# Rotary embedding on one core: all transfers of x on one DMA ring, in the order of the work

## The chip, the core and the metric

One core of a Trainium2 chip runs the kernel. The metric is device time in microseconds (us) of one execution; the kernel before has a median of 161.87 us over three runs (161.72 to 161.93).

## The reference

x is float32 of shape (16, 512, 1024): 16 batches, 512 positions, 16 heads of 64 columns. cos and sin are (512, 32).

```python
x = x.reshape(batch, seq, num_heads, head_dim)
x1, x2 = x[..., :half_dim], x[..., half_dim:]
cos = cos[None, :, None, :]
sin = sin[None, :, None, :]
rotated = np.concatenate([x1 * cos - x2 * sin,
                          x1 * sin + x2 * cos], axis=-1)
```

33.55 MB are read and 33.55 MB written.

## The kernel before

**Tiles.** A slab is two batches' worth of x, 4.19 MB: 128 partitions with 8 rows of 1024 floats each (8192 floats a partition). There are eight slabs, 0 to 7. Two neighbours make a pair, and three places in on-chip memory hold a pair each, so slabs 6 and 7 reuse the place of slabs 0 and 1. `here(s, n)` is the place of `n` slabs from slab `s` on, `there(t, s, n)` the same slabs in the input or output.

**Loads.** SyncE issues them, on its own ring (L65 in `load`, and L83). In program order: load 0, load 1, slabs 2-3 as two transfers (even partitions, then odd), then slabs 4-5 as one transfer of 8.39 MB (L84). None of these has to wait. Load 6 and load 7 are written behind store 0 and store 1 and wait for them, since they overwrite their places.

**Tables.** ScalarE issues the loads of cos and sin (L78). GpSimd casts them to bf16 (L99), TensorE spreads them over the partitions (L106), VectorE and ScalarE copy the result into two bf16 tables.

**Work on a slab.** It goes in passes: one pass for most slabs, two for slab 0, three for slab 7. ScalarE casts the slab to bf16 in place (`cast`, which calls `copy`, L138), VectorE does two multiplications with the tables (L152) and one addition with the halves swapped (L155), ScalarE copies the result back to float32 in place (`copy` again). ScalarE's copies are kept in the order in which they are written: the cast of the next slab comes ahead of the copy back of this one, and all casts of slab 7 come ahead of the copy back of slab 6. So its order is cast 0 in two parts, cast 1, copy 0 in two parts, cast 2, copy 1, cast 3, copy 2, cast 4, copy 3, cast 5, copy 4, cast 6, copy 5, cast 7 in three parts, copy 6, copy 7 in three parts.

**Stores.** ScalarE issues them on its own ring, between its copies: stores 0 to 3 singly (L69 in `store`), slabs 4-5 as two transfers behind copy 5 (L162), slabs 6-7 as one of 8.39 MB at the end (L69).

An engine works off its own instructions in order. A transfer that waits for a copy or for another transfer makes its issuing engine wait; a transfer that is issued runs by itself. So the loads of slabs 0 to 5 are on SyncE's ring from the start, and the stores come in from ScalarE's ring as they are ready.

Of the kernel before, what the change touches and what calls it, by code (L numbers as in the profile page):

```python
# [2 lines left out]

# [4 lines left out]


@with_exitstack  # L10
def kernel(
    ctx: ExitStack,
    tc: tile.TileContext,
    x: bass.AP,
    cos: bass.AP,
    sin: bass.AP,
    num_heads: int,
    out: bass.AP,
):
    nc = tc.nc  # L20
    P = nc.NUM_PARTITIONS

    batch, seq, dim = x.shape
    nh = num_heads
    hd = dim // nh
    half = hd // 2
    bf16 = mybir.dt.bfloat16
    f32 = mybir.dt.float32

    nb = 2  # L30
    nslabs = batch // nb
    rpp = nb * seq // P
    W = rpp * dim
    TP = seq // rpp
    TW = rpp * half

    out_flat = out.rearrange("b s h d -> b s (h d)")

    singles = ctx.enter_context(tc.tile_pool(name="singles", bufs=1))
    pairs = ctx.enter_context(tc.tile_pool(name="pairs", bufs=3))  # L40
    psum = ctx.enter_context(tc.tile_pool(
        name="psum", bufs=1, space=bass.MemoryType.PSUM))


    def view(t, offset, *dims):
        return dataclasses.replace(t, offset=t.offset + offset,
                                   ap=[t.ap[0], *[list(d) for d in dims]])

    places = [pairs.tile([P, 2 * W], f32, tag="pair", name="pair") for _ in range(3)]


    def here(s, n=1):
        return view(places[s // 2 % 3], s % 2 * W, (1, n * W))


    def there(t, s, n=1):
        return bass.AP(tensor=t.tensor, offset=t.offset + s // 2 * 2 * P * W + s % 2 * W,  # L60
                       ap=[[2 * W, P], [1, n * W]])


    def load(s, n=1):
        nc.sync.dma_start(out=here(s, n), in_=there(x, s, n))  # L65


    def store(s, n=1):
        nc.scalar.dma_start(out=there(out_flat, s, n), in_=here(s, n))  # L69


    load(0)


    cos_sb = singles.tile([TP, TW], f32, tag="cos_sb")
    sin_sb = singles.tile([TP, TW], f32, tag="sin_sb")
    for t, src in ((cos_sb, cos), (sin_sb, sin)):
        nc.scalar.dma_start(out=t, in_=bass.AP(  # L78
            tensor=src.tensor, offset=src.offset, ap=[[TW, TP], [1, TW]]))

    load(1)
    for p in range(2):
        nc.sync.dma_start(out=here(2, 2)[p::2], in_=there(x, 2, 2)[p::2])  # L83
    load(4, 2)  # L84


    pick = singles.tile([TP, 4 * P], bf16, tag="pick")
    nc.gpsimd.memset(pick, 0.0)  # L88
    for h in range(2):
        for g in range(2):  # L90
            part = view(pick, (2 * h + g) * P, (TP // 2, 2 * P // TP), (1, TP // 2))
            nc.gpsimd.affine_select(  # L92
                out=part, in_=part, compare_op=mybir.AluOpType.not_equal,
                fill=1.0 - 2.0 * g, base=-h, pattern=[[0, 2 * P // TP], [-2, TP // 2]],
                channel_multiplier=1)

    tab1 = singles.tile([TP, 2 * TW], bf16, tag="tab1")
    for i, t in enumerate((cos_sb, sin_sb)):
        nc.gpsimd.tensor_copy(out=view(tab1, i * TW, (1, TW)), in_=t)  # L99

    accs, tabs = [], []
    for h in range(2):
        acc = psum.tile([P, 2 * rpp * hd], f32, tag=f"acc{h}", name="acc")
        for i in range(2):
            for f in range(2):
                nc.tensor.matmul(  # L106
                    view(acc, i * rpp * hd + f * half, (hd, rpp), (1, half)),
                    view(pick, (2 * h + i * f) * P, (1, P)),
                    view(tab1, i * TW, (half, rpp), (1, half)),
                    start=True, stop=True)  # L110
        accs.append(acc)
        tabs.append(singles.tile([P, 2 * rpp * hd], bf16, tag=f"tab{h}", name="tab"))
    nc.vector.tensor_copy(out=tabs[0], in_=accs[0])  # L113

    passes = []
    for s in range(nslabs):
        r = 0  # L120
        for n in {0: (4, 4), nslabs - 1: (4, 2, 2)}.get(s, (rpp,)):
            passes.append((s, r, n))
            r += n


    def halves(u):
        s, r, n = u
        t = here(s).bitcast(bf16)
        return [view(t, (2 * r + i * n) * dim, (1, n * dim)) for i in range(2)]


    def cast(u):
        s, r, n = u
        copy(halves(u)[0], view(here(s), r * dim, (1, n * dim)))


    def copy(out, in_):
        tc.keep_in_program_order(nc.scalar.copy(out=out, in_=in_))  # L138


    ahead = list(passes)
    for _ in range(2):
        cast(ahead.pop(0))
    copy(tabs[1], accs[1])
    cast(ahead.pop(0))
    for i, u in enumerate(passes):
        s, r, n = u
        while ahead and len(passes) - len(ahead) < (i + 2 if s < nslabs - 2 else len(passes)):
            cast(ahead.pop(0))
        lo, up = halves(u)  # L150
        for t, a in ((up, 0), (lo, rpp * hd)):
            nc.vector.tensor_mul(  # L152
                out=t, in0=lo,
                in1=view(tabs[s % 2], a + r * hd, (hd, n), (0, nh), (1, hd)))
        nc.vector.tensor_add(  # L155
            out=up, in0=up, in1=view(lo, half, (hd, n * nh), (-half, 2), (1, half)))

        copy(view(here(s), r * dim, (1, n * dim)), up)
        if r + n == rpp:
            if s == 5:  # L160
                for p in range(2):
                    nc.scalar.dma_start(out=there(out_flat, 4, 2)[p::2], in_=here(4, 2)[p::2])  # L162
            elif s == 7:
                store(6, 2)
            elif s < 4:
                store(s)
            if s < 2:
                load(s + 6)


# [1 line left out]
_INS = ['x', 'cos', 'sin', 'num_heads']  # L172
_OUTS = [((16, 512, 16, 64), 'float32')]

_NUMBERS = {'num_heads': 16}


# [26 lines left out]
```

## Time and profile before

| | before |
|---|---|
| median of 3 runs | 161.87 us (161.72 to 161.93) |
| the profiled execution | 161.8 us, span 160.0 us |
| ScalarE busy | 114.3 us (71%) |
| VectorE busy | 107.9 us (67%) |
| TensorE busy | 2.0 us (1%) |
| GpSimd busy | 2.6 us (2%) |
| HBM read, written | 33.69 MB, 33.55 MB |
| mean over the span | 420 GB/s |
| a full cast or copy of a slab on ScalarE | 7.02 us |
| a full multiplication or addition on VectorE | 4.42 us |
| issue of a store on ScalarE | 0.34 us |

The span runs from the first to the last instruction of the profiled execution; its own time is 1.8 us longer. Busy times count work, not the issuing of transfers. Times within the profile are counted from the start of the span. Queue q1 is SyncE's ring, q10 ScalarE's.

### The profile page before, as it was taken

The numbers are of one execution on the slowest core, as the hardware profiler recorded it, in microseconds if no ns is written. First come the engines' busy times: TensorE is split into PE (matmuls) and PEld (weight loads), VectorE is DVE, ScalarE is ACT, GpSimd is POOL, SyncE is SP. The second block draws the span as 40 slices with busy tenths as digits, with TensorE's granted clock in tenths as the row PEclk, the third lists the DMA queues.
The fourth block names the chain that finished last, engine by engine and source line by source line (L and its number), as shares of the span: only waits on it lengthen the run. The fifth ranks groups of instructions, "written<-read, shape, count | busy, mean of one in ns | idle before, by whom it ended". The sixth has DMA issues, their size and how long they took to land.

```text
span 160.0 us, 167 instructions
## 1 busy us (share of the span) xinstructions
PE 2.0 (1%) x8; PEld 1.0 (1%) x8; DVE 107.9 (67%) x34; ACT 114.3 (71%) x24; POOL 2.6 (2%) x11
## 2 busy tenths in 40 slices
PE   0001300000000000000000000000000000000000
PEld 0000100000000000000000000000000000000000
DVE  0000499999951999799889979998999998000000
ACT  3006959993089989998998999999879999500000
POOL 4000000000000000000000000000000000000000
DMA  7999999699599999999999999999997999989966
GB/s 262 401 401 410 426 491 524 262 524 524 254 401 410 606 426 393 393 393 393 467 451 393 434 483 393 401 500 410 393 590 328 524 393 393 524 360 426 524 262 262
DMA packets 1920, 67.24 MB, mean 420 GB/s; under 512 B 256, under 2 KB 384, under 8 KB 384
## 3 DMA queue, kind: packets, MB, share of 16 engines
q1 hardware_dynamic: 880, 33.55, 49.5%
q10 hardware_dynamic: 1040, 33.69, 48.7%
HBM read 33.69 MB, written 33.55 MB: 420 GB/s over the span
## 4 chain that ended last, share of the span: by engine, by line
ACT 52%; DMA 26%; issue 5%; ACTq 1%; SPq 1%; another core or an unknown queue 0%
ACT pair L138 52%; DMA pair<-in_x_dram 26%; ACTq L162 1%; ACTq L69 1%; SPq L65 0%; SPq L83 0%; ACTq L138 0%
## 5 line engine op out<-in xcount | busy, mean ns | idle before, releaser
L138 ACT CAST pair<-pair 128x8192 bf16<-128x8192 f32 (+5 forms) x22 | 112.1, 5155 | 21.9 <-DMA pair<-in_x_dram 19.8
L152 DVE TENSOR_TENSOR pair<-pair,tab 128x8192 bf16<-128x8192 bf16 (+2 forms) x22 | 71.4, 3259 | 9.3 <-ACT pair L138 8.9
L155 DVE TENSOR_TENSOR pair<-pair 128x8192 bf16<-128x8192 bf16 (+2 forms) x11 | 35.8, 3260 | 0.3
L113 DVE CAST tab<-acc 128x1024 bf16<-128x1024 f32 x1 | 1.2, 1225 | 18.3 <-PE acc L106 18.3
L138 ACT ACT_TABLE_LOAD x1 | 1.3, 1283 | 2.0 <-issue 2.0
L106 PE MATMUL acc<-tab,pick 64*128 64x256 bf16 x8 | 2.0, 403 | 17.1 <-POOL tab L99 17.1
L106 PEld LDWEIGHTS <-pick 64*128 64x128 bf16 x8 | 1.0, 127 | 17.6 <-issue 15.6
L92 POOL TENSOR_SCALAR_AFFINE_SELECT pick<-pick 64x128 bf16<-64x128 bf16 x4 | 1.1, 303 | 0.1
L138 ACT CAST tab<-acc 128x1024 bf16<-128x1024 f32 x1 | 1.0, 1004 | 0.0
L99 POOL CAST tab<-cos_sb 64x256 bf16<-64x256 f32 x1 | 0.4, 391 | 9.5 <-DMA cos_sb<-in_cos_dram 9.5
L88 POOL MEMSET pick<- 64x512 bf16 x1 | 0.5, 519 | 0.3 <-POOLq L185 0.3
L99 POOL CAST tab<-sin_sb 64x256 bf16<-64x256 f32 x1 | 0.4, 396 | 4.9 <-DMA sin_sb<-in_sin_dram 4.9
L185 POOL MEMSET const-float32-0.0<- 128x1 f32 x1 | 0.1, 104 | 0.2 <-issue 0.2
L185 POOL MEMSET const-bfloat16-1.0<- 128x1 bf16 x1 | 0.1, 107 | 0.0
L185 POOL MEMSET const-uint8-127<- 128x1 uint8 x1 | 0.1, 107 | 0.0
L185 POOL MEMSET const-float32-1.0<- 128x1 f32 x1 | 0.1, 104 | 0.0
## 6 DMA issues: line engine op xcount, KB each, us to landing
pair<-in_x_dram SPq DMA_DIRECT2D x4, 4096.0 KB, 22.5
out_dram<-pair ACTq DMA_DIRECT2D x4, 4096.0 KB, 32.8
cos_sb<-in_cos_dram ACTq DMA_DIRECT2D x1, 64.0 KB, 11.1
sin_sb<-in_sin_dram ACTq DMA_DIRECT2D x1, 64.0 KB, 15.8
pair<-in_x_dram SPq DMA_DIRECT2D x3, 42.2
out_dram<-pair ACTq DMA_DIRECT2D x3, 21.0
```

The lines of the kernel that those rows point to most:

```text
L69: nc.scalar.dma_start(out=there(out_flat, s, n), in_=here(s, n))
L88: nc.gpsimd.memset(pick, 0.0)
L92: nc.gpsimd.affine_select(out=part, in_=part, compare_op=mybir.AluOpType.not_equal, fill=1.0 - 2.0 * g, base=-h, pattern=[[0, 2 * P // TP] ...
L99: nc.gpsimd.tensor_copy(out=view(tab1, i * TW, (1, TW)), in_=t)
L106: nc.tensor.matmul(view(acc, i * rpp * hd + f * half, (hd, rpp), (1, half)), view(pick, (2 * h + i * f) * P, (1, P)), view(tab1, i * TW, ( ...
L113: nc.vector.tensor_copy(out=tabs[0], in_=accs[0])
L138: tc.keep_in_program_order(nc.scalar.copy(out=out, in_=in_))
L152: nc.vector.tensor_mul(out=t, in0=lo, in1=view(tabs[s % 2], a + r * hd, (hd, n), (0, nh), (1, hd)))
L155: nc.vector.tensor_add(out=up, in0=up, in1=view(lo, half, (hd, n * nh), (-half, 2), (1, half)))
L162: nc.scalar.dma_start(out=there(out_flat, 4, 2)[p::2], in_=here(4, 2)[p::2])
L185: nc = _bacc.Bacc("TRN2", target_bir_lowering=False, num_devices=1)
```

## The change

Loads and stores of x are all issued by SyncE, so they all go through one ring, and they are kept in the order in which they are written. Store 0 stands ahead of the load of slabs 4-5. The order is: load 0, load 1, slabs 2-3 in two transfers, store 0, load 4-5, store 1, load 6, store 2, load 7, store 3, slabs 4-5 stored in two transfers, store 6-7. Loads 6 and 7 stood behind stores 0 and 1 in the program and stand behind stores 1 and 2 now. ScalarE issues only the tables. The copies, the multiplications and the places are what they were.

```diff
     def load(s, n=1):
-        nc.sync.dma_start(out=here(s, n), in_=there(x, s, n))
+        tc.keep_in_program_order(nc.sync.dma_start(out=here(s, n), in_=there(x, s, n)))
 
     def store(s, n=1):
-        nc.scalar.dma_start(out=there(out_flat, s, n), in_=here(s, n))
+        tc.keep_in_program_order(
+            nc.sync.dma_start(out=there(out_flat, s, n), in_=here(s, n)))
...
     load(1)
     for p in range(2):
-        nc.sync.dma_start(out=here(2, 2)[p::2], in_=there(x, 2, 2)[p::2])
-    load(4, 2)
+        tc.keep_in_program_order(
+            nc.sync.dma_start(out=here(2, 2)[p::2], in_=there(x, 2, 2)[p::2]))
...
             if s == 5:
                 for p in range(2):
-                    nc.scalar.dma_start(out=there(out_flat, 4, 2)[p::2], in_=here(4, 2)[p::2])
+                    tc.keep_in_program_order(nc.sync.dma_start(
+                        out=there(out_flat, 4, 2)[p::2], in_=here(4, 2)[p::2]))
             elif s == 7:
                 store(6, 2)
             elif s < 4:
                 store(s)
-            if s < 2:
-                load(s + 6)
+            if s < 3:
+                load(*((4, 2), (6,), (7,))[s])
```

## The prediction

> **What bounds the kernel now.** I read the table of DMA queues first, because the digits of the DMA row are nearly all 9.
>
> ```profile
> q1 hardware_dynamic: 880, 33.55, 49.5%
> q10 hardware_dynamic: 1040, 33.69, 48.7%
> HBM read 33.69 MB, written 33.55 MB: 420 GB/s over the span
> ```
>
> q1 carries SyncE's loads, q10 ScalarE's stores and tables. The packets of both fill 49.5 + 48.7 = 98.2% of 160.0 us, that is 157.1 us on each of the 16 DMA engines. The table of windows shows where the other 2.9 us lie (columns after the width: PE, PEld, DVE, ACT, POOL busy, clock, DMA share, GB/s; a packet is counted whole where it begins, so short windows overshoot).
>
> ```profile
> 1.60:1.70 0.10, 0.00 (x0) 0.02 (x1) 0.00 (x0) 0.00 (x0) 0.10 (x2) 1.00 0.00 0
> 1.70:2.20 0.50, 0.00 (x0) 0.08 (x1) 0.00 (x0) 0.21 (x1) 0.50 (x3) 1.00 3.75 1049
> 24.00:28.00 4.00, 0.00 (x0) 0.00 (x0) 4.00 (x3) 4.00 (x1) 0.00 (x0) 1.00 1.21 524
> 28.00:32.00 4.00, 0.00 (x0) 0.00 (x0) 3.96 (x3) 4.00 (x2) 0.00 (x0) 1.00 0.61 262
> 36.00:40.00 4.00, 0.00 (x0) 0.00 (x0) 3.97 (x2) 1.27 (x1) 0.00 (x0) 1.00 1.36 524
> 46.00:70.00 24.00, 0.00 (x0) 0.00 (x0) 17.77 (x5) 23.59 (x4) 0.00 (x0) 1.00 1.01 437
> 158.50:158.70 0.20, 0.00 (x0) 0.00 (x0) 0.00 (x0) 0.00 (x0) 0.00 (x0) 1.00 0.02 0
> 158.70:160.00 1.30, 0.00 (x0) 0.00 (x0) 0.00 (x0) 0.00 (x0) 0.00 (x0) 1.00 0.00 0
> ```
>
> The first packet begins at 1.7 us, the last near 158.6: 156.9 us that packets fill entirely. The engines of the chip's DMA never stand still; this is one stream, and the order in which its bytes go cannot shorten it. Only packets that took longer than their bytes need can. The rate without trouble is 524 GB/s at share 1.21, so 433 GB/s at share 1. Loads alone (24 to 28) have it, and so has the mixed stretch (46 to 70: 437 at 1.01). Three places show more time for the same bytes. 36 to 40 has 1.36 where 24 to 28 has 1.21 for 524 GB/s: 0.15 x 4 = 0.6 us. 0 to 4 has 0.77 (page, first slice, 262 GB/s) where 28 to 32 has 0.61: 0.6 us, the first bytes of the run. 12 to 16, beside the tables, has 1.02 at 410 GB/s where 48 to 52 has 0.95: 0.3 us. 67.24 MB at 433 GB/s is 155.3 us; with 0.6 + 0.6 + 0.3 it is 156.8 of the 157.1 counted, so 0.3 us is unassigned.
>
> The chain of waits puts ScalarE first; its end says why that is an accident.
>
> ```profile
> ACT 52%; DMA 26%; issue 5%; ACTq 1%; SPq 1%; another core or an unknown queue 0%
> ```
> ```profile
> 108.53 7.01 ACT L138 CAST pair<-pair 128x8192 f32<-128x8192 bf16 x1
> 115.58 1.22 ACTq L162 DMA_DIRECT2D out_dram<-pair  x2
> 116.83 21.34 ACT L138 CAST pair<-pair 128x4096 bf16<-128x4096 f32 x7 [1.29 <-issue]
> 138.21 0.34 ACTq L69 DMA_DIRECT2D out_dram<-pair  x1
> ```
> ```profile
> DMA to landing us min/median/max: 14.7/19.2/23.7
> ```
>
> That is ScalarE's timeline at the end, and the landings of the two stores at L162: issued at 115.58 and 116.11, landed at 130.3 and 139.8. So when the last store is issued at 138.21, the stream has work until about 139.3. From issue to first byte takes 1.0 us at the run's start (0.74 to 1.7), so ScalarE's last copy and the stream meet: both bound the end. The last store lands at 159.2 (issue 138.21 + 21.0).
>
> **The change, part by part.** A slab of 4.19 MB takes 9.67 us: from 130.3 to 159.2 three slabs land (9.64 each), from 139.8 two (9.70).
>
> ScalarE no longer issues seven DMAs: five x 0.34 at L69 and 1.22 for the two at L162, 2.9 us. This shortens ScalarE's chain, not the stream, so alone it is worth nothing.
>
> The stream in its new order, counted from the landing of the first half of slabs 2-3, which the change leaves alone (issued 1.63, 31.3 us to landing: 32.9). Each slab adds 9.67 us: the second half 42.6 (before, it shared with store 0: cast 2 began at 44.49), store 0 52.3, load 4-5 71.6 (before: cast 4 at 73.41), store 1 81.3, load 6 90.9, store 2 100.6, load 7 110.3, store 3 120.0, stores 4-5 129.6 and 139.3, store 6-7 158.6. Thirteen slabs are 125.7 us. Before, the same bytes took 159.2 - 32.9 = 126.3; the 0.6 between them is the excess of 36 to 40.
>
> That holds if SyncE hands over each transfer, 1.0 us ahead of use, before the queue has run out. A full cast or copy is 7.02 us. Store 0 is ready at 37.3 as before, the queue lasts to 42.6. Cast 2 and copy 1: 42.6 + 14.0 = 56.6 for store 1, queue to 71.6. Load 6, behind it, needs store 0's landing (52.3): no wait. Store 2 is ready at 70.7, queue to 90.9. Load 7 needs store 1's landing, so SyncE stands from 71.0 to 81.3, with stores 3 to 7 behind it; load 6 and store 2 cover that to 100.6. Slabs 4-5 at 71.6 give store 3 at 85.7 (queue to 110.3), and cast 5, copy 4, cast 6, copy 5 give 113.8 for stores 4-5 (queue to 120.0). Cast 6 wants load 6 at 99.8 (there at 90.9), cast 7 load 7 at 113.8 (there at 110.3). The last seven pieces of 21.34 us end at 135.2; the queue lasts to 139.3, a margin of 3.1 us after the lead, where before there was none. The smallest cover is this one and load 7's 3.5 us; if load 7 came over 6.6 us late, ScalarE would set the end, us for us.
>
> What the trace does not show is a queue that turns from loads to stores within itself, seven times here. The bounds are 0 and 0.6 us a turn. 0: from 46 to 70 the two queues alternate packet by packet at 437 GB/s and share 1.01, and transfers of one kind follow each other in a queue 9.64 to 9.70 us apart, with no gap. 0.6: the only place in the run where a store comes in behind loads alone, 36 to 40. I take 0, because the same engines turn there at every packet. And the 0.6 itself? It arises when the second queue comes into work beside the first, or because the first store is slow wherever it stands. Later stores, and the last one after 139, show none. In the changed kernel the queue is never empty at that point, and store 0 waits in it for 4 us; so I take the 0.6 as gone, and keep 0 to 0.6 for the range. A gain beyond it has only the unassigned 0.3 us to come from.
>
> One rule speaks against the change. The Trainium skill ("DMA: Bandwidth & Descriptors", Anatomy of one DMA) fits a fixed cost of about 2.0 us to each transfer of the GpSimd path; exposed at each of the ten transfers after the second half of slabs 2-3, it would add an estimated 20 us. The landings just named, at bare bandwidth, speak against that for a filled queue.
>
> The sum is 160.0 - 0.6 = 159.4 us of span, plus the 1.8 that the profiled execution has outside it (161.8 - 160.0): 161.2. That execution is 0.07 under the median of 161.87, so against the median: 161.3.
>
> **The rivals.**
>
> *Nothing moves* (161.9). The 0.6 belongs to the first store of the run and stays. For it: one event can't tell the queue from the first write. Against it: only that store 0 now stands in line for 4 us with its queue awake, which is why I put it behind the first case and not level with it. It leaves every landing from store 0 on 0.6 later. The Trainium skill (the same page, Issuing engines are not separate DMA queues) says that DMAs from any engine run on the same 16 engines and that several issuers save only issue time, which is this rival's result; the trace agrees in the rate of 46 to 70 and cannot place the 0.6.
>
> *Turns inside a queue cost* (163.7, slower). Each of the four turns from loads to stores (after slabs 2-3, 4-5, 6 and 7) takes the 0.6 of 36 to 40: 4 x 0.6 - 0.6 = 1.8 us more than now; with the three turns back too, 7 x 0.6 - 0.6 = 3.6, so 165.5. It decides from about 0.23 us a store turn on (0.6 paid now plus 0.32, over four). [...] Against it: the alternation of 46 to 70.
>
> *The queue runs dry* (162.3 or more). Load 7's wait for store 1 holds all later stores. A transfer handed over to an empty queue costs the 1.0 us from issue to first byte, so 161.3 + 1.0 for one, and each us that it comes later is a us more. It decides when store 1 lands after 99.6, which my count puts 18 us away; a store 0 ready after 41.6 (now 37.3) is the other such place.
>
> **How the numbers follow.** Gone 0.42, nothing moves 0.26, turns cost 0.23, dry 0.09. A measurement of this kernel can tell about 0.2%, 0.32 us, from no change; the three runs of before lie within 0.21. Faster by more: the first case and a little of the second, 0.44. Within it: 0.25. Slower: 0.31, the last two less a turn cost too small to see. The range begins at 161.3 less the unassigned 0.3 and a tenth of scatter, 160.9, and ends at the four turns' 163.7 with a tenth, 163.8. It leaves out seven dear turns and most of a dry queue, under 0.2. The two likeliest cases alone are 160.9 to 162.0.
>
> **What would show it.** Right: the whole traffic of x stands under one queue; the window in which the first stores begin has share 1.21 for 524 GB/s; cast 2 begins near 42.6 and cast 4 near 71.7; ScalarE ends near 135; the last landing is near 158.6. Nothing moves: the window of the first stores has 0.15 too much, and all landings behind it are 0.6 later. Turns: excess after every turn, landings late by steps. Dry: windows with the DMA share under 0.9 between 42 and 139. Wrong in kind: the order of landings is not that of the list above, or ScalarE's last copy ends later than 138.

## The result, and the profile after

The changed kernel takes 162.41 us (median of 16 runs) where the kernel before takes 161.84 beside it (16 runs): ratio 1.0047, interval 1.0025 to 1.0069. So it is slower; its median is 0.57 us longer, and its runs lie wider: 161.92 to 164.33, against 161.54 to 162.24. A ratio, here and below, is not the quotient of the two medians and leaves out executions more than 1.5% above the fastest of their kernel; of the profiles used, only that of `warm` is of such an execution. The profiled execution took 162.2 us with a span of 160.4 (before: 161.8 and 160.0).

The table of DMA queues of the changed kernel:

```profile
q1 hardware_dynamic: 1760, 67.11, 97.7%
q10 hardware_dynamic: 160, 0.13, 0.2%
HBM read 33.69 MB, written 33.55 MB: 419 GB/s over the span
```

All of x is on q1. The packets fill 97.9% of 160.4 us, 157.0 us, where they filled 157.1 before. So the sixteen DMA engines together have neither more nor less to do, and still the span is 0.4 us longer.

The windows of the changed kernel, columns as in the prediction:

```profile
24.00:28.00 4.00, 0.00 (x0) 0.00 (x0) 4.00 (x3) 4.00 (x1) 0.00 (x0) 1.00 1.21 524
36.00:40.00 4.00, 0.00 (x0) 0.00 (x0) 3.97 (x2) 1.30 (x1) 0.00 (x0) 1.00 1.36 524
46.00:70.00 24.00, 0.00 (x0) 0.00 (x0) 19.13 (x5) 24.00 (x4) 0.00 (x0) 1.00 1.05 455
```

The 0.15 too much from 36 to 40 is still there, though no second queue comes in. From 46 to 70 the rate is 455 / 1.05 = 433 GB/s, as before.

The shares of the chain of waits, ScalarE's timeline from cast 2 on, and SyncE's last stores:

```profile
DMA 35%; ACT 28%; DVE 11%; issue 8%; ACTq 2%; SPq 0%
```
```profile
43.22 27.78 ACT L140 CAST pair<-pair 128x8192 bf16<-128x8192 f32 x4 [5.92 <-DMA pair<-in_x_dram]
72.27 55.66 ACT L140 CAST pair<-pair 128x8192 bf16<-128x8192 f32 x10 [1.27 <-DMA pair<-in_x_dram]
...
113.92 1.65 SPq L164 DMA_DIRECT2D out_dram<-pair  x2
...
129.32 7.21 ACT L140 CAST pair<-pair 128x4096 f32<-128x4096 bf16 x3 [1.39 <-DVE pair L157]
...
136.55 0.35 SPq L71 DMA_DIRECT2D out_dram<-pair  x1
```

ScalarE's part of the chain is down from 52% to 28%. It ends 1.7 us earlier than before (136.5 for 138.2), so the last store waits in a queue that still has work. The last store lands at 136.55 + 23.0 = 159.55, before at 159.2. Nothing in these views says where the 0.35 us comes from: shares and rates are means over the sixteen engines.

The DMA engines can be told apart at the end. The last packet of each is one of 64 KB, 2.42 us long. If all sixteen begin one in the same half microsecond, the share of that window is 4.84; one engine alone is 0.30. So a share divided by 0.30 counts the engines that begin their last packet there. Last packets before:

```profile
155.50:156.00 0.50, 0.00 (x0) 0.00 (x0) 0.00 (x0) 0.00 (x0) 0.00 (x0) 1.00 0.00 0
156.00:156.50 0.50, 0.00 (x0) 0.00 (x0) 0.00 (x0) 0.00 (x0) 0.00 (x0) 1.00 4.84 2097
156.50:157.00 0.50, 0.00 (x0) 0.00 (x0) 0.00 (x0) 0.00 (x0) 0.00 (x0) 1.00 0.00 0
```

and after:

```profile
155.50:156.00 0.50, 0.00 (x0) 0.00 (x0) 0.00 (x0) 0.00 (x0) 0.00 (x0) 1.00 0.60 262
156.00:156.50 0.50, 0.00 (x0) 0.00 (x0) 0.00 (x0) 0.00 (x0) 0.00 (x0) 1.00 3.32 1442
156.50:157.00 0.50, 0.00 (x0) 0.00 (x0) 0.00 (x0) 0.00 (x0) 0.00 (x0) 1.00 0.91 393
```

Before, all sixteen begin between 156.0 and 156.5. After, 2 begin sooner, 11 in that window, and 3 later. The transfer is done when the last engine is. Three theories follow. Theory A: where the ring turns from loads to stores (a turn, from here on), some engines fall behind; each has a fixed share of the bytes and never catches up; the mean stays and the last engine ends the run. Theory B: it costs to hold load 4-5 back. Theory C: it costs to hand each transfer over through SyncE, whatever its direction.

### The profile page after: what moved, and what is told of

Its sections match the earlier page's. It is cut to its first block, busy times and chain, and to the rows that moved or that the text cites. A ratio compares the mean times of both kernels' runs of the same rounds, so it can differ in the third digit from the quotient of the medians.

```text
span 160.4 us, 175 instructions
## 1 busy us (share of the span) xinstructions
PE 2.0 (1%) x8; PEld 1.0 (1%) x8; DVE 107.9 (67%) x34; ACT 114.0 (71%) x24; POOL 2.6 (2%) x11
## 3 DMA queue, kind: packets, MB, share of 16 engines
q1 hardware_dynamic: 1760, 67.11, 97.7%
## 4 chain that ended last, share of the span: by engine, by line
DMA 35%; ACT 28%; DVE 11%; issue 8%; ACTq 2%; SPq 0%
DMA pair<-in_x_dram 35%; ACT pair L140 28%; DVE pair L154 10%; ACTq L202 1%; DVE pair L157 1%; SPq L66 0%; SPq L71 0%; ACTq L140 0%
## 6 DMA issues: line engine op xcount, KB each, us to landing
pair<-in_x_dram SPq DMA_DIRECT2D x3, 34.5
```

## Experiments

Times are medians in us; ratios are against the kernel before, run beside it on the same chip. The changed kernel has four turns.

**Quarters by partitions, alternating or not** (`turns`, `pieces`). In the changed kernel, stores 0 to 2 and the loads behind them as four transfers each:

```diff
+    def quarter(q, t, s, n=1):
+        place, far = here(s, n)[q::4], there(t, s, n)[q::4]
+        tc.keep_in_program_order(nc.sync.dma_start(
+            out=place if t is x else far, in_=far if t is x else place))
...
+                for q in range(4):
+                    quarter(q, out_flat, s)
+                    quarter(q, x, *((4, 2), (6,), (7,))[s])
```

In `pieces` the stores and the loads have a loop each.

> One ring as in the changed kernel, but stores 0 to 2 and loads 4-5, 6 and 7 go as quarters (every fourth partition) that alternate: 13 turns from loads to stores in the ring instead of 4. Theory A (each such turn inside a ring delays the DMA engines that lag behind by 0.1 to 0.2 us, and the last engine ends the run): 9 turns more, +0.9 to +1.8 on the changed kernel's 162.4, so 163.3 to 164.2, and the marks of the last landing spread over more than 1 us. Theory B (what costs is that load 4-5 is held back) and theory C (a cost of each transfer handed over by SyncE that is independent of its direction): B 162.4, C the same time as the run with quarters that don't alternate.

> The same quarters, but all four of a store ahead of all four of the load behind it: 4 turns as in the changed kernel, with 18 transfers more. A: 162.4, as the changed kernel. B: 162.4. C: later than 162.4 by 18 times the cost of a transfer, as late as the run with alternating quarters.

Measured 223.65 and 212.12 us, which tells nothing of the theories. The DMA row of the page of `turns`:

```profile
DMA  7999998899897000989999940008800089848994
```

The zeros are stretches in which the sixteen engines are nearly idle. The waits of that run show a new one:

```profile
DVE pair L160 <- DMA out_dram<-pair: 11.2, 2, 6.9
```

VectorE waits 11.2 us for stores of quarters, which it never does in the changed kernel. Longer still are the waits of VectorE and ScalarE for each other, 126 us in all; they stand in `pieces` too (115 us), which has no such wait for a store. What sets them off was not followed up. Below, the pieces are cut by columns.

**Load 4-5 at the front** (`early45`): one ring, 3 turns.

```diff
+    load(4, 2)
...
-            if s < 3:
-                load(*((4, 2), (6,), (7,))[s])
+            if 0 < s < 3:
+                load(s + 5)
```

> One ring as in the changed kernel, but load 4-5 back at the front, as before the change: 3 turns from loads to stores. A: 162.2 to 162.4, a little under the changed kernel and over the 161.84 of before. B: 161.8, the order being that of before. C: 162.4.

Measured 162.26, ratio 1.0024 (1.0010 to 1.0038): slower than before, and by its ratio between before and the changed kernel, whose interval it overlaps. B alone would have given back all of it. A fits, but this run can't say how much of the rest is the fourth turn and how much the place of load 4-5. Last packets:

```profile
155.50:156.00 0.50, 0.00 (x0) 0.00 (x0) 0.00 (x0) 0.00 (x0) 0.00 (x0) 1.00 1.81 786
156.00:156.50 0.50, 0.00 (x0) 0.00 (x0) 0.00 (x0) 0.00 (x0) 0.00 (x0) 1.00 2.72 1180
156.50:157.00 0.50, 0.00 (x0) 0.00 (x0) 0.00 (x0) 0.00 (x0) 0.00 (x0) 1.00 0.30 131
```

6, 9 and 1 engines: more windows than before, but one engine after 156.5 where the changed kernel has three.

**Two rings, load 4-5 held back** (`held`): the kernel before, with

```diff
-        nc.sync.dma_start(out=here(s, n), in_=there(x, s, n))
+        tc.keep_in_program_order(nc.sync.dma_start(out=here(s, n), in_=there(x, s, n)))
...
-    load(4, 2)
...
+            elif s == 0:
+                nc.scalar.dma_start(out=there(out_flat, 0)[16:], in_=here(0)[16:])
+                tc.keep_in_program_order(
+                    nc.sync.dma_start(out=there(out_flat, 0)[:16], in_=here(0)[:16]))
+                load(4, 2)
```

> Two rings as before the change, but load 4-5 is held back: SyncE stores 16 partitions of slab 0 itself and issues load 4-5 behind that (ScalarE stores the other 112). A: 161.8 to 161.9, as before, since the stores have a ring of their own. B: 162.4, as the changed kernel. C: 161.9.

Measured 170.36, ratio 1.0537 (1.0512 to 1.0562): no theory had this. The timeline of this run at cast 4 and at the last store:

```profile
81.77 13.94 ACT L136 CAST pair<-pair 128x8192 bf16<-128x8192 f32 x2 [9.19 <-DMA pair<-in_x_dram]
...
146.56 0.34 ACTq L69 DMA_DIRECT2D out_dram<-pair  x1
```

On two rings the late load runs beside the stores. Cast 4 begins at 81.77, 8.4 us later than before (73.41); the last store is issued at 146.56, 8.4 later than before (138.21); the median is 8.4 over that of before beside it (161.94). So this run doesn't separate the order from the ring. It shows that holding load 4-5 back, which one ring bears, was dear on two: on one ring load 4-5 landed 34.5 us after its issue and cast 4 begins at 72.27.

**Turns counted, two ways.** First, quarters by columns (`turns13`, `turns4`), all 128 partitions in each, with the same loops as above:

```diff
+    def quarter(q, t, s, n=1):
+        w = n * W // 4
+        place = view(places[s // 2 % 3], s % 2 * W + q * w, (1, w))
+        far = bass.AP(tensor=t.tensor, ap=[[2 * W, P], [1, w]],
+                      offset=t.offset + s // 2 * 2 * P * W + s % 2 * W + q * w)
...
```

> One ring as in the changed kernel, but stores 0 to 2 and loads 4-5, 6 and 7 go as quarters cut by columns (all 128 partitions in each), store and load quarters alternating: 13 turns from loads to stores instead of 4. Theory A (at a turn the engines that lag finish their last load packets late, by up to 0.1 to 0.5 us, so the sixteen engines drift apart and the last one ends the run): later than the same quarters with 4 turns, by 0.5 to 1.5 us, with last landings spread over more than 1.2 us. Theory C (a cost of each transfer): same as the run with 4 turns.

> The same column quarters, all four of a store ahead of all four of the load behind it: 4 turns, 18 transfers more than the changed kernel. A: 162.4, as the changed kernel. C: over 162.4, as late as the run with 13 turns.

Measured 163.90 (ratio 1.0137, 1.0124 to 1.0151) and 163.41 (1.0101, 1.0088 to 1.0115). The same pieces in another order: nine turns more cost 0.49 us, just under the 0.5 to 1.5 that A expected, and the fastest run with 13 turns (163.84) is behind the slowest with 4 (163.47). Last packets with 13 turns:

```profile
156.50:157.00 0.50, 0.00 (x0) 0.00 (x0) 0.00 (x0) 0.00 (x0) 0.00 (x0) 1.00 1.21 524
157.00:157.50 0.50, 0.00 (x0) 0.00 (x0) 0.00 (x0) 0.00 (x0) 0.00 (x0) 1.00 1.81 786
157.50:158.00 0.50, 0.00 (x0) 0.00 (x0) 0.00 (x0) 0.00 (x0) 0.00 (x0) 1.00 1.51 655
158.00:158.50 0.50, 0.00 (x0) 0.00 (x0) 0.00 (x0) 0.00 (x0) 0.00 (x0) 1.00 0.30 131
```

and with 4:

```profile
156.50:157.00 0.50, 0.00 (x0) 0.00 (x0) 0.00 (x0) 0.00 (x0) 0.00 (x0) 1.00 0.30 131
157.00:157.50 0.50, 0.00 (x0) 0.00 (x0) 0.00 (x0) 0.00 (x0) 0.00 (x0) 1.00 3.02 1311
157.50:158.00 0.50, 0.00 (x0) 0.00 (x0) 0.00 (x0) 0.00 (x0) 0.00 (x0) 1.00 1.51 655
```

4, 6, 5 and 1 engines, against 1, 10 and 5: with 13 turns the first engines are earlier and the last later. A had the changed kernel's 162.4 for the run with 4 turns, and it is 1.0 us over that. This goes with the packets: 4352 on q1 for 1760, and 98.3% of the span of 161.5 us, 158.8 us, for 157.0.

Second, whole slabs and fewer turns (`turns2`): load 4-5 at the front, and loads 6 and 7 together behind store 1.

```diff
+    load(4, 2)
...
-            if s < 3:
-                load(*((4, 2), (6,), (7,))[s])
+            if s == 1:
+                load(6)
+                load(7)
```

> One ring, load 4-5 at the front, then store 0, store 1, load 6, load 7, store 2 and on: 2 turns from loads to stores. A: 161.9 to 162.2, under the run with load 4-5 at the front and 3 turns (162.26). C: 162.3, as that run, the number of transfers being the same.

Measured 161.83, ratio 1.0009 (0.9998 to 1.0020): no difference from before that can be told. Last packets:

```profile
155.50:156.00 0.50, 0.00 (x0) 0.00 (x0) 0.00 (x0) 0.00 (x0) 0.00 (x0) 1.00 0.60 262
156.00:156.50 0.50, 0.00 (x0) 0.00 (x0) 0.00 (x0) 0.00 (x0) 0.00 (x0) 1.00 4.23 1835
```

One ring, the same transfers, the same sizes, and no loss is left that can be told. C falls with it: as many transfers go through SyncE as in the changed kernel.

**Both once more** (`again`, `turns2_again`), on one chip.

> The changed kernel once more, beside the run with 2 turns, for a second profile of the spread. A (the engines drift apart at the turns, each time in another way): about 1.005 of before, and the last packets of the engines again begin over more than 0.8 us, where before the change they began within 0.5. If the drift in the first profile was an accident: within 0.5 us, and a time as before.

> The run with 2 turns from loads to stores once more, on the same chip as the changed kernel. A: 0.4 to 0.6 us under the changed kernel, within 0.2% of before, the last packets begin within 0.6 us. Otherwise: the same as the changed kernel.

Measured 162.86 (ratio 1.0056, 1.0034 to 1.0079) and 162.02 (1.0010, 0.9998 to 1.0022), 0.84 apart where A had 0.4 to 0.6; the intervals do not meet. Last packets of the changed kernel in this profile, whose span is 161.2 us:

```profile
155.50:156.00 0.50, 0.00 (x0) 0.00 (x0) 0.00 (x0) 0.00 (x0) 0.00 (x0) 1.00 0.91 393
156.00:156.50 0.50, 0.00 (x0) 0.00 (x0) 0.00 (x0) 0.00 (x0) 0.00 (x0) 1.00 2.72 1180
156.50:157.00 0.50, 0.00 (x0) 0.00 (x0) 0.00 (x0) 0.00 (x0) 0.00 (x0) 1.00 0.60 262
157.00:157.50 0.50, 0.00 (x0) 0.00 (x0) 0.00 (x0) 0.00 (x0) 0.00 (x0) 1.00 0.30 131
157.50:158.00 0.50, 0.00 (x0) 0.00 (x0) 0.00 (x0) 0.00 (x0) 0.00 (x0) 1.00 0.30 131
```

3, 9, 2, 1 and 1 engines. Twelve begin by 156.5 (13 in the first profile), two trail by up to 1.5 us, and the span is 0.8 us over that of the first profile of the same kernel. A drift that differs from run to run would also explain why its runs lie so wide; two profiles don't prove it. The second profile with 2 turns, with a span of 160.5:

```profile
156.00:156.50 0.50, 0.00 (x0) 0.00 (x0) 0.00 (x0) 0.00 (x0) 0.00 (x0) 1.00 3.02 1311
156.50:157.00 0.50, 0.00 (x0) 0.00 (x0) 0.00 (x0) 0.00 (x0) 0.00 (x0) 1.00 1.81 786
```

10 and 6 engines. By the packets' own times they begin over 0.87 us, where A had at most 0.6, and that is hardly less than the 0.92 of the changed kernel's first profile. So the spread of a single profile does not tell two turns from four; the times of many runs do.

The trace also shows where the engines part. It has sixteen landing marks for each transfer, taken here as one an engine. From the first to the last of the sixteen, in us:

| | load 4-5 | load 6 | load 7 | store 3 | store 6-7 |
|---|---|---|---|---|---|
| changed kernel, first profile | 0.59 | 0.64 | 0.89 | 0.91 | 0.88 |
| `again` | 0.80 | 1.13 | 1.69 | 1.69 | 1.67 |
| `turns2` | 0.38 | 0.48 | 0.49 | 0.53 | 0.51 |
| `turns2_again` | 0.60 | 0.69 | 0.78 | 0.87 | 0.87 |

With four turns the spread grows from one load behind a store to the next, and from load 7 on, through all the stores that are left, it stays as it is. In `turns13` it grows over all the turns, from 0.63 to 1.67, and then stays too. Before the change it is 0.41 at the last store. The middle of the sixteen lands there at 158.94 before and at 159.03 and 159.14 in the two profiles of the changed kernel; the last one lands at 159.19, 159.59 and 160.36. So the middle hardly moves, and the last engines end the run, as A has it.

**What the 0.6 us is** (`warm`, `soft_two`, `soft_one`). First the kernel before with an early first write, which the last store overwrites:

```diff
+    nc.scalar.dma_start(out=there(out_flat, 6, 2)[:TP, :TW], in_=cos_sb)
```

> The kernel before, with one more store ahead of all: ScalarE writes the cos table (64 KB) into a part of the output that the last store overwrites. It asks what the 0.6 us of the window from 36 to 40 is. If it is the first write of the run, the window shows 1.21 for 524 GB/s, and the time is up to 0.6 us under before, 161.3. If it is the turn of the engines from loads alone to bulk stores, the window keeps 1.36 and the time stays at 161.9.

Measured 162.08, ratio 1.0015 (1.0006 to 1.0024). The window of the first bulk store, from a profiled execution of 165.68 us:

```profile
36.00:40.00 4.00, 0.00 (x0) 0.00 (x0) 3.97 (x2) 1.87 (x1) 0.00 (x0) 1.00 1.31 508
```

508 / 433 = 1.17 are due: 0.14 x 4 = 0.6 us. So in this execution the excess is there although another write came first, and the median is not the 161.3 that the first write would have meant. The excess goes with the first bulk store. With load 4-5 at the front that store comes 19 us later; the window from 36 to 40 then has 1.21 for 524 GB/s, and the excess stands in the one from 56 to 60 (1.25 in `early45`, 1.32 in `turns2`, here `turns2_again`):

```profile
56.00:60.00 4.00, 0.00 (x0) 0.00 (x0) 3.97 (x2) 4.00 (x2) 0.00 (x0) 1.00 1.35 524
```

Then store 0 as four transfers by columns, on two rings and on one:

```diff
+        w = n * W // (4 if s == 0 else 1)
+        for q in range(n * W // w):
...
```

> The kernel before, with store 0 alone cut into four transfers by columns. It asks whether the 0.6 us of the first turn is tied to a large store coming in: in the run with column quarters and 4 turns that window had no excess (0.98 at 426 GB/s). If it is, the excess of 0.15 in the window of the first stores goes, and the time falls to 161.3 to 161.6. If the size of the store has nothing to do with it: an excess anywhere between 0 and 0.6, and a time as before, 161.8 to 161.9.

> The changed kernel, with store 0 alone cut into four transfers by columns. If the 0.6 us is tied to a large store: no excess in the window of the first stores, and 161.8 to 162.1. If not: 162.4, as the changed kernel.

Measured 162.75 (ratio 1.0043, 1.0011 to 1.0075) and 163.15 (1.0085, 1.0065 to 1.0104): both slower than either expectation. On one ring the window has 1.29 for 524 GB/s, 0.3 us too much. On two rings it is clean:

```profile
36.00:40.00 4.00, 0.00 (x0) 0.00 (x0) 3.97 (x2) 1.52 (x1) 0.00 (x0) 1.00 1.14 492
```

492 / 433 = 1.14: no excess. And the run is slower than before by 0.9 us. Its last packets:

```profile
156.00:156.50 0.50, 0.00 (x0) 0.00 (x0) 0.00 (x0) 0.00 (x0) 0.00 (x0) 1.00 1.51 655
156.50:157.00 0.50, 0.00 (x0) 0.00 (x0) 0.00 (x0) 0.00 (x0) 0.00 (x0) 1.00 1.21 524
157.00:157.50 0.50, 0.00 (x0) 0.00 (x0) 0.00 (x0) 0.00 (x0) 0.00 (x0) 1.00 2.12 918
```

5, 4 and 7 engines. So the excess at the first store can vanish without a gain. Two things went up instead: the packets fill 97.9% of 161.2 us, 157.8 for 157.1, with 432 packets more; and the engines drifted apart, though this kernel has two rings. Drift is therefore not a matter of one ring alone.

## Why the prediction was wrong

It forecast 161.3, faster, and the kernel is slower. That the time lies within its range is luck: the range reached so far up for the sake of a rival that priced another mechanism.

*The stream bounds the kernel*: right. The packets fill 157.0 us after and 157.1 before.

*The hand-over by SyncE covers everything*: right. Cast 2 began at 43.22 (42.6 was worked out), cast 4 at 72.27 (71.6), ScalarE ended at 136.5 (135.2; it waited 1.4 us for VectorE's addition), and the last store was in the queue at 136.55, before the work ahead of it ran out (stores 4-5 landed at 140.28). The rival of a dry queue had no part in it.

*The 0.6 us is gone*: wrong, first failing step; without it the forecast would have been no change. The 0.6 stood in the changed kernel at its old size. It is not tied to the second queue, nor to the first write, and it isn't fixed: in `again` the window has 1.21 at 508 GB/s, 0.15 us too much, and in `soft_two` none.

*Turns inside a queue cost 0*: wrong, and this step set the sign. It rested on windows at full rate, which are means over sixteen engines; a mean can't show that one of them falls behind. The rival with the turns named the right place and the wrong form. It priced a turn at 0.6 us for all engines, 163.7. Measured, the mean stays (157.0 for 157.1 us of packets), the engines drift apart, and with whole slabs on one ring the time rises with the number of turns: 1.0009 and 1.0010 with two, 1.0024 with three, 1.0047 and 1.0056 with four. From two turns to four that is 0.6 to 0.75 us, some 0.3 a turn, of 4 to 8 MB on either side; the smaller pieces of `turns13` cost 0.49 / 9 = 0.05 a turn. Two and four are clearly apart. The interval of three overlaps both neighbours', and from two to four the place of load 4-5 changes as well; only `turns13` against `turns4` changes the turns alone. With shorter packets four turns come out higher, 1.0085 in `soft_one` and 1.0101 in `turns4`.

*Nothing moves*: the interval of the changed kernel excludes 1, so no, though it was right in that the 0.6 stayed in the first profile. The rule that it cites from the Trainium skill ("DMA: Bandwidth & Descriptors", Issuing engines are not separate DMA queues), that several issuers save only issue time, agrees with `turns2`, where one ring does what two did (1.0009).

What stays open is why an engine falls behind at a turn while others don't, and why two rings, whose packets alternate, left the engines within 0.41 us before the change and 1.10 us apart in `soft_two`. No run here looks inside an engine. No version tried beats the kernel before; the one with two turns is level with it.

## What to carry to other kernels

Where transfers bound a kernel, look at the engines one by one, not only at their mean: the windows around the last packets show whether they end together. If they don't, the slowest one is the time, however full the mean is. On one ring it paid here to group loads with loads and stores with stores as far as the waits allow: that won back the loss. One ring in place of two was worth nothing by itself.

## What the runs showed of the hardware

- At the first turn from loads to bulk stores the mean excess ran from 0 (`soft_two`) over 0.15 (`again`) to 0.6 us (before, the changed kernel, `warm`), without a bearing on the time that could be seen.
- Shorter packets cost: with 2592 more on q1, 162 an engine, the packets of `turns4` took 158.8 - 157.0 = 1.8 us more, about 11 ns for each packet added; the span grew by 1.1 us.
- An engine that has fallen behind stays behind to the end of the run: in `again` the sixteen landings lie 1.69 us apart at load 7 and 1.67 at the last store, 48 us later, and two engines began their last packet up to 1.5 us after the main group.
